# Two residual inputs: from Pool in one go to DVE in twelve pieces

## The chip, the core and the metric

The kernel runs on one core of a Trainium2 chip. A core has five engines that run their own instruction queues in order: TensorE (PE, matmuls and transposes), VectorE (DVE), ScalarE (ACT), GpSimd (Pool) and SyncE (SP), which issues most DMAs. They wait for each other through semaphores. The metric is the device time of one launch in microseconds (us).

## What is computed

Two blocks on a sequence of 256 tokens by 1024 channels, all in float32. The first (a convolution mixer and a mixture of 32 experts) ends in an RMS norm with weights `final_g`; its result is the input of the second. The second is two attention layers, each followed by a layer norm over the residual:

```python
for layer in range(DEPTH_2):
    if layer < N_A:
        y = mla_mixer(x, mla_w_in[layer], ...)
    else:
        if shared is None:
            shared = moba_shared_kv(x, moba_w_kv, cos_b, sin_b)
        y = moba_mixer(x, shared[0], shared[1], shared[2], moba_w_in[j], moba_w_o[j], cos_b, sin_b)
    x = layer_norm(ALPHA * x + y, ln_g[layer], ln_b[layer])
```

So each layer's input `x` is used twice: as the operand of its projections, and once more at its end as the residual `ALPHA * x`. The first layer's input (`x3` here) is the normed stream times `final_g`; the second's (`x4`) is the normed stream times `ln_g` plus `ln_b`.

## The kernel before

Tokens lie in two tiles of 128 (index `t`), channels in eight chunks of 128 (index `k`). Matmuls are made exact enough by splitting each float32 operand in a high part (rounded to the type `fp32r`) and the rest: `split` and `scaled_split` (L282 to L287) let ACT write the high part and DVE subtract it from the source. A product is then three matmuls: high by high, low by high, high by low. The weights are split in the same way, 1024 columns at a time, as `sh` (ACT) and `sl` (DVE); they are planned some chunks ahead of their use.

Each engine's order is set when the program is built, by a scheduler that the dependencies steer; `tc.issue_after(ins)` puts what is written in its block behind `ins`, where both are on the same engine.

The stages that matter here, in order of time:

- `to_channels` (L1175): PE transposes a token tile chunk by chunk into PSUM, the norm's weights are applied per channel on the way out (`xf`, by ACT for odd chunks, by DVE at L1192 for even ones), and `split` makes `xh` and `xl`. For the first layer this reads `x2` (the tile is called `x3` in the trace's program, shown as `x`), for the second `x4n`. So the projections don't need `x3` or `x4` themselves.
- First layer: keys' and values' latent rows (`pk`), their norm, the rotated key part `kr` (L1418 to L1423, copied at L1447 and transposed by PE at L1450), then six chunks of latent queries. `latent_q(i)` is one chunk: 24 matmuls into `pq`, `cqh` by ACT, `cql` by DVE (L287), the square `sqq` by ACT (L1431), which Pool adds up (L1433).
- Behind the latent queries `x2` is multiplied by `final_g` (`fg`, all rows alike) on Pool, L1455, two instructions of 128 x 1024. They stand behind Pool's norm power `kv_norm` in order. This is the residual of the first layer, read at its end (`out_norm`, L1392).
- Second layer: `x4n` is the normed stream; `to_channels` brings it to `xh`, `xl`, and the value projection `values(0)` begins as chunks arrive. Pool makes `x4` of `x4n` with two multiplies (L1546) and two adds (L1547) of 128 x 1024 by the rows `gb`.
- Then the key loop, eight chunks `m`: 24 matmuls, and `rope_t`: ACT copies the result to `raw`, `split` makes its high and low part (in `cqh`, on DVE the low part), and `rope_end` rotates the chunk before: two matmuls `pr`, DVE's `t1 = pr * sin` (L1260, shown as `t`), Pool's `raw = raw * cos` (L1261), DVE's sum `kn` (L1265). PE goes on with the next chunk ahead of `pr`.
- `values(1)`, and the second layer's attention and output.

The residual parts as written before:

```python
    with tc.issue_after(kv_norm.ins):
        for t in range(NT):
            nc.gpsimd.tensor_mul(x2[:, t, :], x2[:, t, :], fg[:, 0, :])
```

```python
    for t in range(NT):
        nc.gpsimd.tensor_mul(x4[:, t, :], x4n[:, t, :], gb[:, 0, :])
        nc.gpsimd.tensor_add(x4[:, t, :], x4[:, t, :], gb[:, 1, :])
```

Of the kernel before, what the change touches and what calls it, by code (L numbers as in the profile page):

```python
# [15 lines left out]
NT = 2  # L16
D = 1024
KD = 8
# [7 lines left out]
EPS = 1e-6  # L26
# [3 lines left out]
KVL = 256  # L30
# [5 lines left out]
V_C, V_AB, V_MIX, V_FFN, V_BIN, V_BDW, V_LNG, V_LNB, V_QN, V_KN, V_FIN = 0, 8, 56, 64, 72, 88, 96, 104, 112, 118, 120  # L36
# [5 lines left out]
T_MASK, T_COSA, T_SINA, T_COSB, T_SINB, T_R32, T_R64, T_COSK, T_SINK, T_N = (  # L42
    0, 256, 512, 768, 1024, 1280, 1408, 1536, 1600, 1664)
# [38 lines left out]
CQ_FIRST = 2  # L82
# [103 lines left out]
def build(tc, A, out, dbg=None, stop=None):  # L186
    nc = tc.nc
# [4 lines left out]
    def dump(name, t):  # L192
        if name in dbg:
            nc.sync.dma_start(dbg[name], t)
# [55 lines left out]
    vec = const.tile([P, V_ROWS], F32, name="vec")  # L250
    x2 = pre.tile([P, NT, D], F32, name="x2")
# [23 lines left out]
    def rsqrt(dst, ss, scale, eps):  # L275

        n = dst.shape[-1]
        nc.vector.tensor_scalar(dst, ss, scale, eps, op0=OP.mult, op1=OP.add)
        return nc.gpsimd.tensor_tensor(out=dst, in0=dst, in1=expn[:, :n], op=OP.pow)

    def split(hi, lo, src, eng=None):
        a = nc.scalar.copy(hi, src)  # L282
        return a, (eng or nc.vector).tensor_sub(lo, src, hi.bitcast(F32))  # L283

    def scaled_split(hi, lo, src, g):
        a = nc.scalar.activation(hi, src, AF.Identity, scale=g)
        return a, nc.vector.scalar_tensor_tensor(lo, src, g, hi.bitcast(F32), op0=OP.mult, op1=OP.subtract)  # L287
# [149 lines left out]
    for q in range(4):  # L437
        w = W.get()
        for i in range(2):
            m = 2 * q + i  # L440
# [76 lines left out]
    i = 0  # L517
# [107 lines left out]
    for k in range(KD):  # L625
# [3 lines left out]
        if k in (1, 2):  # L629
            h = k - 1  # L630
            c = slice(512 * h, 512 * h + 512)
# [174 lines left out]
    for t in range(NT):  # L806
        c = (P + 2 * E) * t
# [215 lines left out]
    x2 = xq.tile([P, NT, D], F32, name="x3")  # L1023
# [86 lines left out]
    for j in (1, 0):  # L1110
        for t in range(NT):
            last = scatter(done, t, False, True, (j,))

    pw = pme.tile([P, 512], F32, name="pw", tag="pgu")
    for i in range(WARM):
        with tc.issue_after(last.ins):
            last = mm(pw, ident, g2b[:, 0:512], True, True)
# [45 lines left out]
    def tab(a, n=T):  # L1163
        return tbl[:, a:a + n]
# [51 lines left out]
    def chunk_t(kk, xh, xl, pat=None):  # L1216
        wh, wl = S.get()
        if pat is not None:
            wh, wl = wh.rearrange(pat), wl.rearrange(pat)
        return proj_t(lambda k: wh[:, k], lambda k: wl[:, k], kk, xh, xl)  # L1220
# [28 lines left out]
    def rope_end():  # L1249

        dst, raw, rh, rl, rot, cos, sin = ropes.pop(0)
        pr = ps.tile([P, T], F32, name="pr", tag="pt", bufs=2)
        if rh is None:
            mm(pr, rot, raw, True, True)
        else:
            mm(pr, rot, rh, True, False)
            mm(pr, rot, rl, False, True)
        del rh, rl
        t1 = tw.tile([P, T], F32, name="t1", tag="xf")
        nc.vector.tensor_mul(t1, pr, sin)  # L1260
        nc.gpsimd.tensor_mul(raw, raw, cos)  # L1261
        n = P // len(dst)
        for i, d in enumerate(dst):
            r = slice(n * i, n * i + n)
            nc.vector.tensor_add(d, raw[r, :], t1[r, :])  # L1265
# [7 lines left out]
    def rope_t(dst, pin, rot, cos, sin):  # L1273

        raw = tw.tile([P, T], F32, name="raw", tag="raw")
        nc.scalar.copy(raw, pin)
        rh = rl = None
        if rot.dtype == F32R:
            spare.append(spare.pop(0))
            rh, rl = (cqh[:, 2 * spare[0] + i] for i in range(2))  # L1280
            split(rh, rl, raw)
        ropes.append((dst, raw, rh, rl, rot, cos, sin))
        if len(ropes) > 1:
            rope_end()

    mask = tab(T_MASK)

# [125 lines left out]
    for t in range(NT):  # L1413
        nc.scalar.activation(junk, pk[t][:, :KVL], AF.Square, accum_out=sts[:, 4 + t:5 + t])
        nc.scalar.copy(kr[:, t].rearrange("p a b -> p (a b)"), pk[t][:, KVL:KVL + RD])
        kv_norm = rsqrt(sts[:, 6 + t:7 + t], sts[:, 4 + t:5 + t], 1.0 / KVL, EPS)
        nc.vector.tensor_scalar(ckn[:, t, :], pk[t][:, :KVL], sts[:, 6 + t:7 + t], None, op0=OP.mult)
    sink = tab(T_SINK, 64).rearrange("p (t a b) -> p t a b", t=NT, a=2)  # L1418
    kr2v = kr2.rearrange("p t (a b) -> p t a b", a=2)
# [7 lines left out]

    def latent_q(i):
        pq = chunk_t(KD, xh, xl)
        scaled_split(cqh[:, i, :], cql[:, i, :], pq, vec[:, V_QN + i:V_QN + i + 1])  # L1430
        nc.scalar.activation(sqq[:, i, :], pq, AF.Square)  # L1431
        if 0 < i < 5:
            nc.gpsimd.tensor_add(sqq[:, 0, :], sqq[:, 0, :], sqq[:, i, :])  # L1433

    for i in range(CQ_FIRST):
        latent_q(i)
# [12 lines left out]
    for t in range(NT):  # L1449
        nc.tensor.transpose(ptk[0:96, P * t:P * t + P], kr4[:, t].rearrange("p a b -> p (a b)"), ident)  # L1450
    for i in range(CQ_FIRST, 6):
        latent_q(i)
    with tc.issue_after(kv_norm.ins):
        for t in range(NT):
            nc.gpsimd.tensor_mul(x2[:, t, :], x2[:, t, :], fg[:, 0, :])  # L1455
    dump("x3", x2)

    kR = ptk[64:96, :].unsqueeze(1).to_broadcast([RD, 4, T])
# [83 lines left out]
        to_channels((t,), x4n, v2[:, 0:8], v2[:, 16:24], xh, xl)  # L1542
    x4 = big("x4", shape=(NT, D))
    gb = rows(A["ln_g_2"][0:1, :], A["ln_b_2"][0:1, :])
    for t in range(NT):
        nc.gpsimd.tensor_mul(x4[:, t, :], x4n[:, t, :], gb[:, 0, :])  # L1546
        nc.gpsimd.tensor_add(x4[:, t, :], x4[:, t, :], gb[:, 1, :])  # L1547
    dump("x4", x4)


    r64 = cql[:, 0, 0:P]
# [9 lines left out]
    rotation[:] = ROT_B  # L1561
    values(0)
    for m in range(8):
        rope_t([kn[:, m, :]], chunk_t(KD, xh, xl), r64, tab(T_COSB), tab(T_SINB))
    values(1)
    rope_flush()
    ogh, ogl = big("ogh", F32R), big("ogl", F32R)
# [121 lines left out]
```

## Time and profile before

| | us |
|---|---|
| median of 3 runs (945.17 to 946.70) | 946.23 |
| the profiled execution | 945.95 |
| its span in the trace | 944.3 |
| PE busy | 869.0 (92%) |
| DVE busy | 526.6 (56%) |
| ACT busy | 361.2 (38%) |
| Pool busy | 58.2 (6%) |

Times in the rows below are counted from the span's start. A row of a timeline gives start, duration, engine, line, operation, output and inputs with their shapes, how many instructions are merged in it (x2), and in brackets how long the engine stood idle before and what released it. Shares over the whole span say little here, since the stages have different limits; the second block begins near 636 us.

### The profile page before, as it was taken

The page shows a single profiled execution, that of the slowest core. Times are in us where ns is not written, and L with a number is a line of the kernel's source. Part 1 is how long each engine was busy: PE and PEld are TensorE (multiplying, and loading weights), DVE is VectorE, ACT ScalarE, POOL GpSimd, SP SyncE. Part 2 cuts the span into 40 slices and gives each one's busy share as a digit, 9 for nine tenths or more (in the row PEclk, how much of TensorE's full clock was granted, in tenths as well). Part 3 has the DMA queues.
Part 4 walks back from the last instruction along what each step waited for, and adds up shares of the span by engine and source line. Part 5 has one row for each costly group of instructions (what it writes and reads, how often), then busy time and mean ns, then how long its engine had stood idle before and what let it go on. Part 6 is the DMA issues. An engine that isn't in the chain of part 4 may idle for free. (4 is left out here: it accounts for less than half of the span.)

```text
span 944.3 us, 15434 instructions
## 1 busy us (share of the span) xinstructions
PE 869.0 (92%) x6227; PEld 609.6 (65%) x6227; DVE 526.6 (56%) x1243; ACT 361.2 (38%) x788; POOL 58.2 (6%) x62
## 2 busy tenths in 40 slices
PE   4899879899999999999699999878999996999996
PEld 1597346665565555656356555538988874988975
DVE  2699965623343333334223342357777868758876
ACT  1455645412122121212012121145766735655761
POOL 0000210100000000000000000003100004110112
PEclk9899989999999999999899999999999998999998
DMA  9994968789999999999999999974432441624211
GB/s 372 411 389 191 406 249 317 323 362 426 427 427 428 426 427 426 427 426 430 422 428 425 426 429 425 425 311 159 170 140 91 179 178 45 255 102 179 90 45 45
DMA packets 23580, 289.44 MB, mean 307 GB/s; under 512 B 2736, under 2 KB 3408, under 8 KB 6096
## 3 DMA queue, kind: packets, MB, share of 16 engines
q1 hardware_dynamic: 21872, 282.29, 72.4%
q10 hardware_dynamic: 1632, 6.11, 1.8%
q8 instruction: 51, 0.84, 0.4%
q14 instruction: 25, 0.20, 0.1%
HBM read 287.34 MB, written 1.05 MB: 305 GB/s over the span
## 5 line engine op out<-in xcount | busy, mean ns | idle before, releaser
L197 PE MATMUL pgu<-w,xg 128*64 128x256 f32 x2048 | 233.5, 381 | 4.2 <-DMA w<-in_moe 4.2
L197 PEld LDWEIGHTS pgu<-w,xg 128*64 128x64 f32 x2048 | 145.6, 137 | 90.1 <-issue 20.8
L197 PE MATMUL pys<-w,hTe 128*64 128x512 f32 x512 | 116.1, 594 | 5.4 <-DMA w<-in_moe 2.5
L283 DVE TENSOR_TENSOR sl<-w,sh 128x1024 fp32r<-128x1024 f32 (+2 forms) x82 | 98.0, 1204 | 20.4 <-ACT sh L282 19.2
L282 ACT CAST sh<-w 128x1024 fp32r<-128x1024 f32 (+2 forms) x82 | 81.4, 1001 | 48.9 <-PE pj L197 46.0
L1012 DVE SCALAR_TENSOR_TENSOR yt<-pys,gs,g2b 64x512 f32<-64x512 f32 x64 | 48.0, 750 | 87.2 <-PE pys L197 86.2
L282 ACT CAST yh<-yt 64x512 fp32r<-64x512 f32 x64 | 39.6, 618 | 138.9 <-DVE yt L1012 137.3
L197 PE MATMUL pj<-xh,sh 128*128 128x256 f32 x304 | 86.6, 285 | 0.1
L197 PE MATMUL pj<-xl,sh 128*128 128x256 f32 x304 | 85.5, 281 | 0.0
L197 PE MATMUL pj<-xh,sl 128*128 128x256 f32 x304 | 85.3, 281 | 0.0
L197 PEld LDWEIGHTS pys<-w,hTe 128*64 128x64 f32 x512 | 36.2, 137 | 65.9 <-issue 54.5
L854 DVE TENSOR_TENSOR hid<-pgu,hid 128x256 f32<-128x256 f32 x32 | 13.6, 425 | 97.2 <-ACT hid L853 97.2
L853 ACT ACTIVATE hid<-pgu 128x256 f32<-128x256 f32 x32 | 12.3, 385 | 125.8 <-PE pgu L197 119.7
L197 PEld LDWEIGHTS pj<-xh,sh 128*128 128x128 f32 x304 | 57.1, 188 | 2.2 <-issue 1.6
L197 PEld LDWEIGHTS pj<-xl,sh 128*128 128x128 f32 x304 | 57.0, 188 | 1.8 <-issue 1.7
L197 PEld LDWEIGHTS pj<-xh,sl 128*128 128x128 f32 x304 | 57.1, 188 | 0.8 <-issue 0.8
L411 DVE SCALAR_TENSOR_TENSOR y<-up,wdw,y 128x256 f32<-128x256 f32 x120 | 54.9, 513 | 0.1
L283 DVE TENSOR_TENSOR yl<-yt,yh 64x512 fp32r<-64x512 f32 x64 | 44.0, 687 | 2.2 <-ACT yh L282 0.2
L197 PE MATMUL pu<-hh,wh 128*128 128x256 f32 x128 | 37.4, 292 | 2.7 <-ACT wh L282 2.7
L283 DVE TENSOR_TENSOR wl<-w,wh 128x512 fp32r<-128x512 f32 x48 | 33.2, 702 | 12.0 <-ACT wh L282 10.5
L282 ACT CAST wh<-w 128x512 fp32r<-128x512 f32 x48 | 29.3, 620 | 27.5 <-PE pu L197 20.4
L862 DVE COPY hTe<-pth 128x256 f32<-128x256 f32 x32 | 13.6, 425 | 44.6 <-PE pth L203 40.1
(343 smaller groups left out, 1579.2 us busy)
## 6 DMA issues: line engine op xcount, KB each, us to landing
w<-in_moe SPq DMA_DIRECT2D x95, 2048.0 KB, 32.0
w<-in_wst SPq DMA_DIRECT2D x32, 2048.0 KB, 8.7
w<-in_wst SPq DMA_DIRECT2D x5, 1152.0 KB, 5.1
w<-in_wst SPq DMA_DIRECT2D x2, 1536.0 KB, 11.2
wb<-in_wbd ACTq DMA_DIRECT2D x4, 512.0 KB, 7.0
w<-in_wst SPq DMA_DIRECT2D x2, 1024.0 KB, 22.6
w<-in_moe SPq DMA_DIRECT2D x4, 512.0 KB, 31.2
x<-in_x SPq DMA_DIRECT2D x1, 1024.0 KB, 11.5
```

The costliest lines, as they stand in the source:

```text
L197: ins = nc.tensor.matmul(o, l, r, start=start, stop=stop)
L282: a = nc.scalar.copy(hi, src)
L283: return a, (eng or nc.vector).tensor_sub(lo, src, hi.bitcast(F32))
L411: nc.vector.scalar_tensor_tensor(y[:, m, :], u, wdw[:, m, k:k + 1], y[:, m, :], op0=OP.mult, op1=OP.add)
L853: nc.scalar.activation(hid, pgu[:, 0:256], AF.Silu)
L854: nc.vector.tensor_mul(hid, pgu[:, 256:512], hid)
L862: nc.vector.tensor_copy(hT, pt.rearrange("p (q j s) -> p q j s", q=2, j=2))
L1012: nc.vector.scalar_tensor_tensor(yt[r, :], pys[r, :], gs[r, e % 2:e % 2 + 1], g2b[r, 512 * j:512 * j + 512], op0=OP.mult, op1=OP.mult)
```

## The change

Pool's six instructions of 128 x 1024 go. DVE does the same work in twelve pieces of 128 x 512: four multiplies of `x2`, one behind each of the latent queries 2 to 5, and for `x4` a multiply and an add in turn behind each of the eight keys' splits, with `issue_after` on that split's low part. To that end `rope_t` and `latent_q` now return it.

```diff
@@ rope_t
-        rh = rl = None
+        rh = rl = last = None
         if rot.dtype == F32R:
             spare.append(spare.pop(0))
             rh, rl = (cqh[:, 2 * spare[0] + i] for i in range(2))
-            split(rh, rl, raw)
+            last = split(rh, rl, raw)[1]
         ropes.append((dst, raw, rh, rl, rot, cos, sin))
         if len(ropes) > 1:
             rope_end()
+        return last
@@ latent_q
-        scaled_split(cqh[:, i, :], cql[:, i, :], pq, vec[:, V_QN + i:V_QN + i + 1])
+        a, v = scaled_split(cqh[:, i, :], cql[:, i, :], pq, vec[:, V_QN + i:V_QN + i + 1])
         nc.scalar.activation(sqq[:, i, :], pq, AF.Square)
         if 0 < i < 5:
             nc.gpsimd.tensor_add(sqq[:, 0, :], sqq[:, 0, :], sqq[:, i, :])
+        return v
@@
     for i in range(CQ_FIRST, 6):
-        latent_q(i)
-    with tc.issue_after(kv_norm.ins):
-        for t in range(NT):
-            nc.gpsimd.tensor_mul(x2[:, t, :], x2[:, t, :], fg[:, 0, :])
+        with tc.issue_after(latent_q(i).ins):
+            t, c = (i - CQ_FIRST) // 2, slice(512 * (i % 2), 512 * (i % 2) + 512)
+            nc.vector.tensor_mul(x2[:, t, c], x2[:, t, c], fg[:, 0, c])
@@
-    for t in range(NT):
-        nc.gpsimd.tensor_mul(x4[:, t, :], x4n[:, t, :], gb[:, 0, :])
-        nc.gpsimd.tensor_add(x4[:, t, :], x4[:, t, :], gb[:, 1, :])
-    dump("x4", x4)
+
+    def x4_part(m, after):
+
+        with tc.issue_after(after.ins):
+            t, c = m // 4, slice(512 * (m // 2 % 2), 512 * (m // 2 % 2) + 512)
+            if m % 2:
+                nc.vector.tensor_add(x4[:, t, c], x4[:, t, c], gb[:, 1, c])
+            else:
+                nc.vector.tensor_mul(x4[:, t, c], x4n[:, t, c], gb[:, 0, c])
@@
     for m in range(8):
-        rope_t([kn[:, m, :]], chunk_t(KD, xh, xl), r64, tab(T_COSB), tab(T_SINB))
+        x4_part(m, rope_t([kn[:, m, :]], chunk_t(KD, xh, xl), r64, tab(T_COSB), tab(T_SINB)))
+    dump("x4", x4)
```

The order of instructions on PE, ACT and SP is the same in both programs. On DVE at the latent queries (`x_5219` is `x2`, `rows` is `fg`, a row ending in x2 is two instructions), first before:

```order
L283 TENSOR_TENSOR sl<-w,sh 128x1024 x2
L287 SCALAR_TENSOR_TENSOR cql<-pj,vec,cqh 128x256 x2
L283 TENSOR_TENSOR sl<-w,sh 128x1024 x2
L287 SCALAR_TENSOR_TENSOR cql<-pj,vec,cqh 128x256 x2
L283 TENSOR_TENSOR sl<-w,sh 128x1024
```

Now, in the same place:

```order
L283 TENSOR_TENSOR sl<-w,sh 128x1024 x2
L287 SCALAR_TENSOR_TENSOR cql<-pj,vec,cqh 128x256
L1456 TENSOR_TENSOR x_5219<-x_5219,rows 128x512
L287 SCALAR_TENSOR_TENSOR cql<-pj,vec,cqh 128x256
L1456 TENSOR_TENSOR x_5219<-x_5219,rows 128x512
L283 TENSOR_TENSOR sl<-w,sh 128x1024 x2
L287 SCALAR_TENSOR_TENSOR cql<-pj,vec,cqh 128x256
L1456 TENSOR_TENSOR x_5219<-x_5219,rows 128x512
```

One piece stands directly behind each `cql` of the queries 2 to 5, ahead of the next `cql` or the next weight split. On DVE at the key loop's first steps (`cqh<-raw,cqh` is the low part of the split), before:

```order
L283 TENSOR_TENSOR cqh<-raw,cqh 128x256
L1260 TENSOR_TENSOR t_7156<-pr,tbl 128x256
L1265 TENSOR_TENSOR kn<-raw,t_7156 128x256
L283 TENSOR_TENSOR sl<-w,sh 128x1024
L283 TENSOR_TENSOR cqh<-raw,cqh 128x256
```

Now (`x_7010` is `x4`, `rows` is `gb`):

```order
L283 TENSOR_TENSOR cqh<-raw,cqh 128x256
L1554 TENSOR_TENSOR x_7010<-x4n,rows 128x512
L1260 TENSOR_TENSOR t_7155<-pr,tbl 128x256
L1265 TENSOR_TENSOR kn<-raw,t_7155 128x256
L283 TENSOR_TENSOR sl<-w,sh 128x1024
L283 TENSOR_TENSOR cqh<-raw,cqh 128x256
L1552 TENSOR_TENSOR x_7010<-x_7010,rows 128x512
```

A piece stands between each split of a raw key and the `t` that waits for PE's rotation; the same in all eight steps.

## Rows read from the trace of the kernel before

**Rows 1.** Waits of PE, 640 to 690 us: who for whom, total, times, longest
```profile
PE ptk L1450 <- DVE kr L1447: 2.5, 1, 2.5
PE pj L197 <- ACT sqq L1431: 0.3, 1, 0.3
```

**Rows 2.** Waits of PE, 780 to 850 us
```profile
PE pt L1182 <- DVE xf L1192: 3.8, 2, 2.0
PE pt L1182 <- ACT xf L1190: 2.4, 2, 2.1
PE pj L197 <- DVE xl L283: 1.6, 1, 1.6
```

**Rows 3.** Stretches: length, busy of PE, PEld, DVE, ACT, POOL, clock, DMA share, GB/s
```profile
786.00:796.00 10.00, 2.51 (x10) 1.21 (x8) 9.72 (x7) 2.27 (x7) 9.07 (x4) 0.81 0.06 25
796.00:800.00 4.00, 4.00 (x14) 3.02 (x14) 2.89 (x7) 3.81 (x10) 0.00 (x0) 0.62 0.00 0
800.00:806.00 6.00, 6.00 (x27) 4.87 (x26) 4.87 (x9) 4.71 (x9) 0.00 (x0) 1.00 0.47 147
```

**Rows 4.** Timeline, Pool and DVE, 646.5 to 653 us
```profile
646.82 4.75 POOL L1455 TENSOR_TENSOR x<-x,rows 128x1024 f32<-128x1024 f32 x2 [0.30 <-issue]
646.96 2.37 DVE L1423 TENSOR_TENSOR rows<-rows 128x64 f32<-128x64 f32 x1
...
652.57 0.25 DVE L1447 COPY kr<-rows 128x192 f32<-128x192 f32 x1
```

**Rows 5.** Timeline, Pool and DVE, the transposing stage of `x4n`
```profile
785.48 0.41 DVE L1192 TENSOR_SCALAR xf<-pt,v 128x128 f32<-128x128 f32 x1
785.66 4.72 POOL L1546 TENSOR_TENSOR x<-x4n,rows 128x1024 f32<-128x1024 f32 x2 [2.13 <-PE pj L197]
785.81 4.72 DVE L283 TENSOR_TENSOR xl<-xf,xh 128x128 fp32r<-128x128 f32 x2
...
795.33 0.41 DVE L1192 TENSOR_SCALAR xf<-pt,v 128x128 f32<-128x128 f32 x1
...
797.68 0.41 DVE L1192 TENSOR_SCALAR xf<-pt,v 128x128 f32<-128x128 f32 x1
```

**Rows 6.** Groups of DVE instructions up to 640 us: count, busy, mean ns
```profile
L605 DVE TENSOR_TENSOR x<-x,rg 128x512 f32<-128x512 f32 x3 | 2.0, 688 | 0.0
```

**Rows 7.** Timeline, DVE, Pool and PE, two steps of the key loop, and its last split
```profile
814.39 0.42 DVE L283 TENSOR_TENSOR cqh<-raw,cqh 128x256 fp32r<-128x256 f32 x1
814.88 0.75 POOL L1261 TENSOR_TENSOR raw<-raw,tbl 128x256 f32<-128x256 f32 x1 [2.23 <-DVE cqh L283]
814.91 0.40 PE L197 MATMUL pr<-cqh,cql 128*128 128x256 f32 x2
815.34 0.43 DVE L1260 TENSOR_TENSOR t<-pr,tbl 128x256 f32<-128x256 f32 x1 [0.54 <-PE pr L197]
815.87 0.43 DVE L1265 TENSOR_TENSOR kn<-raw,t 128x256 f32<-128x256 f32 x1
816.21 1.22 DVE L283 TENSOR_TENSOR sl<-w,sh 128x1024 fp32r<-128x1024 f32 x1
...
832.56 0.42 DVE L283 TENSOR_TENSOR cqh<-raw,cqh 128x256 fp32r<-128x256 f32 x1
```

**Rows 8.** Timeline, DVE, latent queries 3 and the weight splits behind
```profile
660.69 0.48 DVE L287 SCALAR_TENSOR_TENSOR cql<-pj,vec,cqh 128x256 fp32r<-128x256 f32 x1 [0.82 <-ACT cqh L286]
661.63 2.91 DVE L283 TENSOR_TENSOR sl<-w,sh 128x1024 fp32r<-128x1024 f32 x2 [0.45 <-ACT sh L282]
```

**Rows 9.** Timeline, DVE and PE: a weight split and PE's first use
```profile
799.02 1.23 DVE L283 TENSOR_TENSOR sl<-w,sh 128x1024 fp32r<-128x1024 f32 x1 [0.66 <-ACT sh L282]
801.39 0.39 PE L197 MATMUL pj<-sl,xh 128*128 128x512 f32 x1
```

**Rows 10.** Timeline, Pool and DVE, queries of the second layer
```profile
881.64 2.82 POOL L1261 TENSOR_TENSOR raw<-raw,tbl 128x256 f32<-128x256 f32 x2 [15.38 <-DVE cqh L283]
882.75 0.42 DVE L283 TENSOR_TENSOR cqh<-raw,cqh 128x256 fp32r<-128x256 f32 x1
```

More of the change, by code (lines that the diff above doesn't have):

```diff
@@ L1415, in build @@
         nc.scalar.copy(kr[:, t].rearrange("p a b -> p (a b)"), pk[t][:, KVL:KVL + RD])
-        kv_norm = rsqrt(sts[:, 6 + t:7 + t], sts[:, 4 + t:5 + t], 1.0 / KVL, EPS)
+        rsqrt(sts[:, 6 + t:7 + t], sts[:, 4 + t:5 + t], 1.0 / KVL, EPS)
         nc.vector.tensor_scalar(ckn[:, t, :], pk[t][:, :KVL], sts[:, 6 + t:7 + t], None, op0=OP.mult)
```

## Prediction

> **What bounds the kernel now.** I read the waits of TensorE (PE) first, then PE's busy time by stretch, then single instructions on DVE and Pool. The change moves work only in two stages of the second block, so the reader should ask of each: is PE, whose matmuls fill it, waiting there, and for whom?
>
> In the stage of the latent queries PE waits once for long, 2.5 us, for the DVE copy of `kr`; a further 0.3 us goes to ACT's `sqq` [rows 1]. In the stage that brings `x4n` to channel layout, PE waits 3.8 us for DVE's `xf`, 2.4 us for ACT's `xf` and 1.6 us for DVE's `xl` [rows 2]. By stretch [rows 3]: from 786 to 796 us PE is busy 2.51 of 10 us and its granted clock is 0.81 on average; from 796 to 800 us it is busy throughout but at 0.62, nearer to its lower level (1.2 GHz) than to the upper (2.4 GHz); from 800 us on it is busy without a break at 1.00. So DVE, which is busy 9.72 of those 10 us, bounds that stretch.
>
> DVE is not short of work capacity there, it is held. [rows 4]: Pool's two multiplies of L1455 run from 646.82 for 4.75 us; the DVE add L1423 on 64 columns, begun 0.14 us later, takes 2.37 us, and the `kr` copy two instructions behind it starts at 652.57. [rows 5]: Pool's L1546 starts at 785.66, and two `xl` subtractions on 128 columns take 4.72 us; when Pool has finished, a pair of channel chunks goes by in (797.68 - 795.33) / 2 = 1.18 us. What is held has both inputs in SBUF; the `xf` that reads PSUM keeps 0.41 us in the midst of it.
>
> **Part 1, Pool's multiply of x3 removed (L1455).** With Pool idle, L1423 ends near 647.2, then comes one weight split of 1.14 us, and `kr` is copied near 648.4, before PE's transposes come up. The 2.5 us wait of [rows 1] goes. Next late would be ACT's `sqq`, 0.3 us. I take 2.5 us; the ends are 2.2 (some of it stays) and 2.8 (both go).
>
> **Part 2, four DVE pieces of x3 added behind `cql`.** A multiply of two SBUF tiles on 128x512 has a row of the same form: 0.688 us [rows 6]. Instructions start 0.08 us before the one ahead has ended in the record (a 1.22 us split at 816.21 on DVE leaves 1.14 to its follower; `kn` of 0.43 at 815.87 has its follower at 816.21 [rows 7]), so a piece fills some 0.60 us. Behind the first and third piece stands a `cql` that today waits 0.82 us for ACT; behind the second and fourth a weight split that waits 0.45 us for ACT [rows 8]. The pieces lie in those waits but for 0.15 us twice, and those splits are made chunks ahead of PE. I take 0. If the cover were gone, 4 x 0.60 = 2.4 us.
>
> **Part 3, Pool's multiplies and adds of x4 removed (L1546, L1547).** Four pairs of chunks take 785.48 to 797.68 = 12.2 us; undisturbed 4 x 1.18 = 4.7. So DVE's chain comes 7.5 us earlier. PE can gain at most its idle 7.49 us plus 4.0 x (1 - 0.62) = 1.5 us of the slow clock: 9.0. What lies between is slack: of the weight splits that PE uses next, the nearest is begun at 799.02, ends 800.25 and is first read at 801.39 [rows 9]: 1.1 us. Thus 7.5 + 1.1 = 8.6 by this split, under the 9.0; I take 8.5, ends 7.5 and 9.0. It supposes that PE keeps the upper clock once its gaps are short; where it doesn't, the low end holds.
>
> **Part 4, eight DVE pieces of x4 added in the key loop.** This is where the change may cost. A step of the loop on DVE is: split of the raw key (`cqh`), wait for PE's rotation `pr`, `t`, `kn`, split of a weight. From 814.39 to 832.56 there are six steps, 3.03 us each [rows 7]. PE has no gap, so here is nothing to win. But its `pr` starts at 814.91 and the second of its two matmuls (near 815.03) needs the split that ends at 814.81: 0.22 us of slack. A DVE loop longer than PE's 3.03 us goes straight to PE.
>
> The piece starts where the split leaves off, 814.39 + 0.33 = 814.72, and lets `t` start at 815.32; `t` starts at 815.34 today. So on DVE alone it is free: it lies in the wait for `pr`. The cost comes by Pool: its `raw` multiply, at 814.88 today, has SBUF inputs too, and now finds DVE busy until 814.72 + 0.69 = 815.41. The same meeting is in [rows 10]: Pool's two `raw` multiplies start at 881.64 in the record and last 2.82 us, to 884.46, while DVE's last two-SBUF instruction ahead ran at 882.75 for 0.42, to 883.17; that leaves 0.65 us for each. So `raw` is done near 816.06 and `kn`, which needs it, starts at 816.10, where it starts at 815.87 today. Then 816.10 + 0.34 + 1.14 = 817.58 for the next split: a step of 3.19 us, 0.16 over PE's. Between the first split and the eighth are seven steps: 7 x 0.16 - 0.22 = 0.9 us. The ends: 0, if `raw` gets through beside the piece; with Pool's own 0.75 us instead of 0.65, 0.26 a step, 1.6 us. Below nothing is excluded, as PE has no gap.
>
> The page "SBUF — State Buffer" of the Trainium skill, section "Who interferes with whom", says that of a DVE instruction with two SBUF inputs and a GpSimd instruction that reads SBUF the first to issue blocks the other for all its length. By that rule the piece, 0.16 us ahead of Pool, blocks Pool and not the reverse, and the sum is the one above; were Pool ahead, it would be the first rival below. The trace agrees in both directions (2.37 us for L1423 behind Pool, 2.82 us for Pool's two behind DVE).
>
> **The sum.** The profiled execution took 945.95 us, its span 944.3. 945.95 - 2.5 - 8.5 + 0.9 = 935.85. It is 0.28 below the median of 946.23, so 936.1 as a median. The order of PE, ACT and SP is the same in both programs, so nothing else is costed. Less than 0.2% (1.9 us) can't be told from no change here.
>
> **The rivals.**
> First, *Pool goes first in the key loop*. Then Pool has 814.88 to 815.63, the piece starts at 815.63, `t` at 816.24, `kn` at 816.77, the next split at 818.25: 3.86 us a step, 0.83 over. 7 x 0.83 - 0.22 = 5.6 us, and 945.95 - 2.5 - 8.5 + 5.6 + 0.28 = 940.8. For it: the margin is 0.16 us. Against: DVE's queue has the piece directly behind the split, and Pool must first be told that the split is done.
> Second, *half the gain goes into a new wait*, the weights: PE comes 11 us earlier, the loads may not. Against: in 786 to 800 us DMA is nearly idle (0.06 and 0.00 [rows 3]), so loads wait for free buffers, and those come free earlier too. It would cost up to half of 8.5: 936.1 + 4.2 = 940.3.
> Third, on the other side, *Pool isn't what holds DVE* in these stages, but something that ends at the same time. Then PE's gaps stay, nothing is gained, and the pieces cost what part 4 gives: 0.9 to 5.6 us, so 947.1 to 951.8, about 949. It decides from the point where the gain is below the key loop's cost, 0.9 us. Against: in two stages, with different tiles, the held instructions are freed as Pool ends, and the next ones run at 1.18 us a pair at once.
> That the change doesn't do what it says is excluded by the order: Pool's six are gone, DVE's twelve stand behind the splits.
>
> **How the numbers follow.** Forecast 936.1 with 0.84; first rival 0.07; second 0.06; third 0.03. The range takes the ends of the terms: 945.95 - 2.8 - 9.0 + 0 + 0.28 = 934.4 and 945.95 - 2.2 - 7.5 + 1.6 + 0.28 = 938.1; with half of the 1.5 us by which the runs shown differ, 933.8 to 938.8. It leaves out the 0.16 of the rivals. Faster by over 0.2%: the forecast and the first two rivals, 0.97; within 0.2%: 0.01; slower: 0.02, most of the third.
>
> **What would show it.** Part 1: PE's wait for `kr` is gone and L1423 is back near 0.2 us. Part 3: no `xl` over 0.5 us, the transposing stage about 8.5 us shorter, the granted clock near 1.00 in it. Part 4: splits of the key loop 3.1 to 3.3 us apart, small PE waits for DVE before `pr`, Pool's `raw` multiplies longer than 1 us. Part 2: no PE wait over 0.5 us between the latent queries. The forecast is wrong if `xl` is still held with Pool idle, if the steps are 3.8 us apart, or if PE waits for weights behind the transposing stage.

## The result, and the profile after

The changed kernel takes 934.86 us (median of 4 runs, 932.90 to 935.73); the kernel before took 945.75 us beside it (945.17 to 946.70). The ratio is 0.9881, with a 95% interval of 0.9863 to 0.9900: faster by 10.9 us between the medians (the ratios here and below come from all runs of the two kernels and aren't quite the quotients of the medians). In two later comparisons the same kernel came to 0.9869 (0.9853 to 0.9886) and 0.9853 (0.9828 to 0.9879). The profiled execution shown here took 935.17 us, with a span of 933.5 us.

To see where the time went I cut both spans at five marks that both traces have: the start of the second block's first norm power on Pool (L279), that of the power ahead of `x4n` (L279), DVE's first and eighth split of a raw key, and its next split, of a query. The figures are differences of start times, in us.

| stretch | before | after | difference | term of the prediction |
|---|---|---|---|---|
| start to the second block's first power | 643.49 | 644.29 | +0.80 | none |
| to `x4n`'s power: latent queries, first attention | 133.60 | 130.36 | -3.24 | parts 1 and 2: -2.5 |
| to the first key split: transposing stage | 34.33 | 25.87 | -8.46 | part 3: -8.5 |
| to the eighth key split: key loop | 21.14 | 21.98 | +0.84 | part 4: +0.9, with the next row |
| to the first query split: values(1) | 14.36 | 14.12 | -0.24 | |
| to the end | 97.38 | 96.88 | -0.50 | none |
| span | 944.3 | 933.5 | -10.8 | -10.1 |

The first row and the last are no work of the change. The first mark stood at 641.9 us in two more executions of the changed kernel, 2.4 us earlier, with the same instructions; and in all the other traces below the last stretch is 96.8 to 97.0 us, so it is before's that is 0.5 long. The rows between them sum to -11.1 us.

The page's first lines, busy time of each engine with its share of the span:

```profile
PE 867.7 (93%) x6227; PEld 609.9 (65%) x6227; DVE 520.6 (56%) x1255; ACT 360.3 (39%) x788; POOL 46.6 (5%) x56
```

DVE has twelve instructions of some 0.6 us more than before and yet 6.0 us less of busy time (526.6 before): it is held less. Pool has six instructions less.

**Latent queries.** The only wait of PE from 640 to 690 us, which answers to [rows 1]:

```profile
PE pj L197 <- ACT sqq L1432: 0.2, 1, 0.2
```

The wait for `kr` is gone. The timeline of DVE shows why (start, duration, engine, line, output and inputs); it answers to [rows 4], with all lines one to two further down:

```profile
647.63 0.21 DVE L1424 TENSOR_TENSOR rows<-rows 128x64 f32<-128x64 f32 x1
647.77 1.22 DVE L283 TENSOR_TENSOR sl<-w,sh 128x1024 fp32r<-128x1024 f32 x1
648.90 0.25 DVE L1449 COPY kr<-rows 128x192 f32<-128x192 f32 x1
...
657.71 0.48 DVE L287 SCALAR_TENSOR_TENSOR cql<-pj,vec,cqh 128x256 fp32r<-128x256 f32 x1 [0.22 <-ACT cqh L286]
658.11 0.68 DVE L1456 TENSOR_TENSOR x<-x,rows 128x512 f32<-128x512 f32 x1
658.71 1.22 DVE L283 TENSOR_TENSOR sl<-w,sh 128x1024 fp32r<-128x1024 f32 x1
```

The add on 64 columns takes 0.21 us where it took 2.37, and `kr` is copied at 648.90 instead of 652.57. The `cql` behind a piece still waits for ACT, 0.22 us where it was 0.82 [rows 8]: the piece lies in that wait.

**Transposing stage.** Waits of PE from 770 to 850 us, which answer to [rows 2]:

```profile
PE pj L197 <- ACT xh L282: 0.9, 1, 0.9
PE pt L1182 <- ACT xf L1190: 0.8, 2, 0.5
```

Then the stretches of [rows 3], with the same columns (length, busy of PE, PEld, DVE, ACT, POOL, clock, DMA share, GB/s):

```profile
786.00:796.00 10.00, 9.97 (x46) 7.68 (x46) 8.59 (x17) 9.39 (x19) 0.00 (x0) 1.00 0.27 90
796.00:800.00 4.00, 4.00 (x37) 4.00 (x36) 2.29 (x3) 2.57 (x5) 0.00 (x0) 1.00 0.99 381
```

and DVE's timeline, which answers to [rows 5]:

```profile
783.02 0.41 DVE L1192 TENSOR_SCALAR xf<-pt,v 128x128 f32<-128x128 f32 x1
...
784.54 0.72 DVE L283 TENSOR_TENSOR xl<-xf,xh 128x128 fp32r<-128x128 f32 x2
...
787.71 0.41 DVE L1192 TENSOR_SCALAR xf<-pt,v 128x128 f32<-128x128 f32 x1
```

Of the 7.8 us of waits that [rows 2] shows the 5.4 for DVE are gone, and of ACT's 2.4 for `xf` 0.8 are left; the 0.9 for ACT's `xh` isn't new: PE waited the same 0.9 us for it before, in a row of that view that [rows 2] doesn't show (`PE pj L197 <- ACT xh L282: 0.9, 1, 0.9`). Two `xl` take 0.72 us together where they took 4.72, and the four pairs go by in 787.71 - 783.02 = 4.69 us instead of 12.2. The granted clock is 1.00 where it was 0.81 and 0.62: PE, with no long gaps ahead, stays at its upper level (2.4 GHz). So 7.8 - 0.8 = 7.0 us of waits went, and 4.0 x (1 - 0.62) = 1.5 us of clock: 8.5, against the 8.46 of the table.

**Key loop.** One step on DVE and Pool, which answers to [rows 7]:

```profile
803.66 0.42 DVE L283 TENSOR_TENSOR cqh<-raw,cqh 128x256 fp32r<-128x256 f32 x1
804.00 0.69 DVE L1552 TENSOR_TENSOR x<-x,rows 128x512 f32<-128x512 f32 x1
804.22 1.07 POOL L1261 TENSOR_TENSOR raw<-raw,tbl 128x256 f32<-128x256 f32 x1 [2.07 <-DVE cqh L283]
804.60 0.42 DVE L1260 TENSOR_TENSOR t<-pr,tbl 128x256 f32<-128x256 f32 x1
805.32 0.42 DVE L1265 TENSOR_TENSOR kn<-raw,t 128x256 f32<-128x256 f32 x1 [0.31 <-POOL raw L1261]
805.67 1.22 DVE L283 TENSOR_TENSOR sl<-w,sh 128x1024 fp32r<-128x1024 f32 x1
806.80 0.42 DVE L283 TENSOR_TENSOR cqh<-raw,cqh 128x256 fp32r<-128x256 f32 x1
```

The piece starts 0.34 us behind the split, and `t` no later than before: 0.94 us behind the split, 0.95 in [rows 7]. Pool's multiply, 0.75 us before, now takes 1.07; `kn` waits 0.31 us for it and starts 1.66 us behind the split instead of 1.48. A step is 806.80 - 803.66 = 3.14 us.

### The profile page after: what moved, and what is told of

Same layout as the page of the kernel before. It is cut to its first block, busy times and chain, and to the rows that moved or that the text cites. A ratio compares the mean times of both kernels' runs of the same rounds, so it can differ in the third digit from the quotient of the medians.

```text
span 933.5 us, 15438 instructions
## 1 busy us (share of the span) xinstructions
PE 867.7 (93%) x6227; PEld 609.9 (65%) x6227; DVE 520.6 (56%) x1255; ACT 360.3 (39%) x788; POOL 46.6 (5%) x56
## 5 line engine op out<-in xcount | busy, mean ns | idle before, releaser
L197 PE MATMUL pgu<-w,xg 128*64 128x256 f32 x2048 | 233.5, 381 | 4.0 <-DMA w<-in_moe 4.0
L197 PEld LDWEIGHTS pgu<-w,xg 128*64 128x64 f32 x2048 | 145.9, 137 | 89.8 <-issue 20.6
L197 PE MATMUL pys<-w,hTe 128*64 128x512 f32 x512 | 116.1, 595 | 5.4 <-DMA w<-in_moe 2.5
L283 DVE TENSOR_TENSOR sl<-w,sh 128x1024 fp32r<-128x1024 f32 (+2 forms) x82 | 95.6, 1173 | 19.0 <-ACT sh L282 17.9
L282 ACT CAST sh<-w 128x1024 fp32r<-128x1024 f32 (+2 forms) x82 | 81.3, 998 | 51.3 <-PE pj L197 47.6
L282 ACT CAST yh<-yt 64x512 fp32r<-64x512 f32 x64 | 39.5, 617 | 139.0 <-DVE yt L1012 137.4
L197 PE MATMUL pj<-xh,sh 128*128 128x256 f32 x304 | 86.7, 285 | 0.0
L197 PE MATMUL pj<-xl,sh 128*128 128x256 f32 x304 | 85.8, 282 | 0.0
L197 PE MATMUL pj<-xh,sl 128*128 128x256 f32 x304 | 85.5, 281 | 0.0
L197 PEld LDWEIGHTS pys<-w,hTe 128*64 128x64 f32 x512 | 36.3, 137 | 65.9 <-issue 54.5
L197 PEld LDWEIGHTS pj<-xh,sh 128*128 128x128 f32 x304 | 57.2, 188 | 1.7 <-issue 1.6
L197 PEld LDWEIGHTS pj<-xl,sh 128*128 128x128 f32 x304 | 57.1, 188 | 1.8 <-issue 1.7
L197 PEld LDWEIGHTS pj<-xh,sl 128*128 128x128 f32 x304 | 57.1, 188 | 0.8 <-issue 0.8
L282 ACT CAST wh<-w 128x512 fp32r<-128x512 f32 x48 | 29.2, 618 | 27.8 <-PE pu L197 21.5
L197 PE MATMUL pu<-hh,wh 128*128 128x256 f32 x128 | 37.2, 291 | 2.7 <-ACT wh L282 2.7
L283 DVE TENSOR_TENSOR wl<-w,wh 128x512 fp32r<-128x512 f32 x48 | 32.8, 693 | 12.2 <-ACT wh L282 11.3
## 6 DMA issues: line engine op xcount, KB each, us to landing
w<-in_wst SPq DMA_DIRECT2D x2, 1536.0 KB, 11.1
```

What stands on the lines that cost most here:

```text
L197: ins = nc.tensor.matmul(o, l, r, start=start, stop=stop)
```

## Experiments

**The two halves alone.** e1 is the changed kernel with Pool's old code for `x4`, e2 the changed kernel with Pool's old code for `x3`. e1, against the kernel after:

```diff
-            if m % 2:
-                nc.vector.tensor_add(x4[:, t, c], x4[:, t, c], gb[:, 1, c])
-            else:
-                nc.vector.tensor_mul(x4[:, t, c], x4n[:, t, c], gb[:, 0, c])
+    for t in range(NT):
+        nc.gpsimd.tensor_mul(x4[:, t, :], x4n[:, t, :], gb[:, 0, :])
+        nc.gpsimd.tensor_add(x4[:, t, :], x4[:, t, :], gb[:, 1, :])
...
```

> Only the four pieces of x3 are on DVE; x4 stays on Pool as before. Theory (Pool's instructions hold DVE's, and each stage pays for itself): the gain of the latent-query stage alone, 3.1 us by the two traces, so 942.6 against 945.75; the transposing stage keeps its xl of over 2 us. Rival (the x3 part gives nothing by itself, since PE waits later anyway): 945.5 to 946.

Measured: 943.51 us (941.57 to 944.05) against 945.64, ratio 0.9964 (0.9948 to 0.9979), 0.9 over the 942.6 expected. The stretch of the latent queries takes 130.37 us, as after (130.36), and PE's waits in the transposing stage stand as in [rows 2]:

```profile
PE pt L1182 <- DVE xf L1192: 3.8, 2, 2.0
PE pt L1182 <- ACT xf L1190: 2.4, 2, 2.1
```

e2, against the kernel after:

```diff
...
-        with tc.issue_after(latent_q(i).ins):
-            t, c = (i - CQ_FIRST) // 2, slice(512 * (i % 2), 512 * (i % 2) + 512)
-            nc.vector.tensor_mul(x2[:, t, c], x2[:, t, c], fg[:, 0, c])
+        latent_q(i)
+    with tc.issue_after(kv_norm.ins):
+        for t in range(NT):
+            nc.gpsimd.tensor_mul(x2[:, t, :], x2[:, t, :], fg[:, 0, :])
```

> Only the eight pieces of x4 are on DVE; x3 stays on Pool as before. Theory: 8.6 us less in the transposing stage, 0.5 to 0.9 more in the key loop, so 937.7 to 938.1. Rival (the two parts share one gain, so that either alone gives nearly all): 935 to 936.

Measured: 937.89 us (936.79 to 938.64), ratio 0.9911 (0.9895 to 0.9928). The transposing stage takes 25.89 us (after: 25.87), the key loop 21.99 (21.98), the latent queries 134.54, 0.9 more than before with a granted clock of 0.92 from 646 to 668 us, and there PE waits nearly as in [rows 1]:

```profile
PE ptk L1452 <- DVE kr L1449: 2.4, 1, 2.4
```

The halves are independent: each gives its own stretch what it has in the whole, and the two shortfalls of the ratio, 0.0036 and 0.0089, sum to 0.0125, the whole's 0.0119 to 0.0147.

**The work on no engine.** e3 leaves both products and the sum out (the residuals are the unscaled streams) and so the transfer of the rows `gb` too:

```diff
-        with tc.issue_after(latent_q(i).ins):
-            ...
+        latent_q(i)
...
-    gb = rows(A["ln_g_2"][0:1, :], A["ln_b_2"][0:1, :])
-    def x4_part(m, after):
-        ...
+    x4 = x4n
```

> Both residual inputs' work is left out on every engine (the norm weights of x3 and x4 are not applied to the residual, and their rows are not loaded for x4). What is left when neither Pool nor DVE has it. Theory: after's time less the key loop's price, 934.9 - 0.6 = 934.3 (933.7 to 934.9), key loop steps 3.03 us. Rival (the DVE pieces cost their full 12 x 0.6 = 7.2 us somewhere): 927 to 928.

Measured: 931.86 us (931.32 to 935.21), ratio 0.9857 (0.9832 to 0.9881). By stretch: latent queries 130.39 us against 130.36 after, so the four `x3` pieces cost nothing (part 2); key loop 21.34 against 21.98, so the `x4` pieces cost some 0.6 us there, of which values(1) gives back 0.2 as in the table above (14.34 us against 14.12). Two more things went that I hadn't expected. The transposing stage takes 25.17 instead of 25.87 us: the two transfers of `gb` that ACT issues amid the transposes (0.33 us of its queue each) are left out, and PE's wait of 0.9 us for `xh` with them. And the second block began 2.0 us earlier, which varies from one execution to the next; it makes up most of the miss in the profiled execution.

**Pool writes only.** e4 is the kernel before with Pool's six instructions replaced by 18 that read nothing and write the same tiles (values that mean nothing); the transfer of `gb`, which nothing reads then, is left out too:

```diff
-            nc.gpsimd.tensor_mul(x2[:, t, :], x2[:, t, :], fg[:, 0, :])
+            for q in range(3):
+                nc.gpsimd.memset(x2[:, t, :], 0.25 + q)
...
-    gb = rows(A["ln_g_2"][0:1, :], A["ln_b_2"][0:1, :])
...
-        nc.gpsimd.tensor_mul(x4[:, t, :], x4n[:, t, :], gb[:, 0, :])
-        nc.gpsimd.tensor_add(x4[:, t, :], x4[:, t, :], gb[:, 1, :])
+        for q in range(6):
+            nc.gpsimd.memset(x4[:, t, :], 0.25 + q)
```

> The kernel before, with Pool's six multiplies and adds replaced by memsets of the same tiles in the same places of Pool's queue (18 of 128 x 1024, so that Pool is busy for about as long): it writes as much but reads nothing; the two inputs' values are left out. Theory (what holds DVE is Pool reading SBUF): L1423 0.2 us, no xl over 0.6 us, PE's waits of 2.5 and 7.8 us gone, time near 934.3. Rival (what holds DVE is Pool being busy, its writes, or something that ends with its instructions): xl and L1423 stay at 2 us and more, time near 945.75.

Measured: 944.72 us in a single execution, where before had 945.64 (944.56 to 948.98); by the count from the second block's first power 301.18 us, against 300.81. Pool and DVE in the two stages:

```profile
644.80 5.43 POOL L1456 MEMSET x<- 128x1024 f32 x6
645.28 0.21 DVE L1423 TENSOR_TENSOR rows<-rows 128x64 f32<-128x64 f32 x1
645.42 1.22 DVE L283 TENSOR_TENSOR sl<-w,sh 128x1024 fp32r<-128x1024 f32 x1
646.55 3.79 DVE L1447 COPY kr<-rows 128x192 f32<-128x192 f32 x1
...
781.38 9.89 POOL L1547 MEMSET x<- 128x1024 f32 x11
781.54 9.87 DVE L1537 TENSOR_SCALAR x4n<-z,mv,rs 128x256 f32<-128x256 f32 x1
791.33 0.39 DVE L1537 TENSOR_SCALAR x4n<-z,mv,rs 128x256 f32<-128x256 f32 x1
791.65 0.28 DVE L283 TENSOR_TENSOR xl<-xf,xh 128x128 fp32r<-128x128 f32 x1
```

The theory's first half holds: the add on 64 columns keeps its 0.21 us and the weight split its 1.22 in the midst of Pool's writes, and no `xl` is held. What I hadn't foreseen is that DVE instructions with one input in SBUF are: the copy of `kr` takes 3.79 us (after: 0.25) and ends 0.11 us behind Pool's last write (645 to 650 us), and of two writes of `x4n` the first takes 9.87 us and ends 0.14 us behind the last of Pool's eleven in that stretch, the second 0.39. So the time didn't fall, for a reason of its own, and the expected 934 was wrong. That Pool isn't what holds DVE (the third rival) falls all the same: which DVE instructions are held changes with what Pool does, and they come free when Pool is done.

**What a step of the key loop pays for.** e5 is the changed kernel without Pool's `raw` multiply in the key loop:

```diff
-        nc.gpsimd.tensor_mul(raw, raw, cos)
+        if not key_loop:
+            nc.gpsimd.tensor_mul(raw, raw, cos)
...
```

> The kernel after, without Pool's multiply of `raw` by the cosine table in the eight steps of the key loop; that factor is left out of the keys, so the work on Pool is missing there and nothing else. My theory: a step is 3.14 us instead of 3.02 because Pool's multiply takes 1.07 us and is done only 0.61 us after the piece is, so that `kn` waits 0.31 us for it. Without it `kn` follows `t` at once, VectorE's work in a step is under TensorE's 3.03 us, the weight splits come 3.02 to 3.05 us apart, and from the first to the seventh `pr` it is 18.1 to 18.3 us instead of 18.70: 0.4 to 0.6 us under the kernel after. Rival: the piece's own 0.60 us on VectorE is the price, however Pool stands; then the splits stay 3.12 to 3.16 us apart and the time is that of after.

Measured: 932.91 us (931.70 to 935.56) against 945.27, ratio 0.9872 (0.9840 to 0.9905); by the time alone this can't be told from after. The trace can tell it: from the first to the eighth split it is 21.06 us (21.97 to 21.98 in three traces of after), 3.01 a step, as fast as before (21.14). One step on DVE:

```profile
804.89 0.42 DVE L283 TENSOR_TENSOR cqh<-raw,cqh 128x256 fp32r<-128x256 f32 x1
805.23 0.68 DVE L1555 TENSOR_TENSOR x<-x4n,rows 128x512 f32<-128x512 f32 x1
805.91 0.42 DVE L1260 TENSOR_TENSOR t<-pr,tbl 128x256 f32<-128x256 f32 x1
806.37 0.43 DVE L1266 TENSOR_TENSOR kn<-raw,t 128x256 f32<-128x256 f32 x1
```

The piece is there, 0.68 us long, and `kn` starts 1.48 us behind the split, as in the kernel before. The kernel before has Pool's multiply and no piece (21.14 us), e5 has the piece and no multiply (21.06 us): neither alone lengthens the loop, the two together do (21.98 us). So DVE's added 0.60 us cost nothing by themselves; the price is the wait for Pool that they bring. The rival, that the piece itself is the price, falls.

e7 puts each piece behind `kn` instead:

```diff
-        x4_part(m, rope_t([kn[:, m, :]], chunk_t(KD, xh, xl), r64, tab(T_COSB), tab(T_SINB)))
+        rope_t([kn[:, m, :]], chunk_t(KD, xh, xl), r64, tab(T_COSB), tab(T_SINB))
+        if m:
+            x4_part(m - 1, last_kn[0])
...
```

> The kernel after with each piece of the key loop put one place later, behind `kn` instead of behind the split of `raw`, so that VectorE's order in a step is `kn`, piece, weight split, sl, t. My theory, that a piece costs by the work of Pool that it meets: Pool's multiply of `raw` now stands beside the next weight split and not behind a piece, but `kn` still waits for the two in turn, so a step is 3.05 to 3.15 us and the time within 0.4 us of the kernel after. Rival: Pool's multiply meets no work that keeps it waiting, VectorE's 2.75 us of work in a step is under TensorE's 3.03, and the steps are 3.02 to 3.03 us with the time about 0.5 us under the kernel after.

Measured: 934.22 us (932.51 to 935.77), ratio 0.9874 (0.9855 to 0.9893), the time of after. The steps from the second on are 3.14 us (3.13 to 3.15); the first, which has no weight split, is 2.43, so the loop is 21.28 us. One of them on Pool and DVE:

```profile
805.80 0.42 DVE L283 TENSOR_TENSOR cqh<-raw,cqh 128x256 fp32r<-128x256 f32 x1
806.13 1.22 DVE L283 TENSOR_TENSOR sl<-w,sh 128x1024 fp32r<-128x1024 f32 x1
806.36 1.60 POOL L1261 TENSOR_TENSOR raw<-raw,tbl 128x256 f32<-128x256 f32 x1 [1.54 <-DVE cqh L283]
807.27 0.42 DVE L1260 TENSOR_TENSOR t<-pr,tbl 128x256 f32<-128x256 f32 x1
808.00 0.42 DVE L1265 TENSOR_TENSOR kn<-raw,t 128x256 f32<-128x256 f32 x1 [0.31 <-POOL raw L1261]
```

As expected, Pool's multiply now lies behind the weight split (1.60 us long, ending 0.61 us after the split does at 807.35), and `kn` waits the same 0.31 us. The rival, steps of 3.02 to 3.03 us, falls. Be the DVE instruction ahead of Pool a piece or a weight split, Pool's multiply ends 0.60 to 0.61 us behind it.

e6 makes each piece 1024 columns wide, the same result twice over:

```diff
-            t, c = m // 4, slice(512 * (m // 2 % 2), 512 * (m // 2 % 2) + 512)
+            t, c = m // 4, slice(0, D)
```

> The kernel after with each piece of `x4` in the key loop 1024 columns wide instead of 512 (each token tile's product and sum are made twice over, the values are the same): twice the added work on VectorE. My theory, a price that starts once VectorE's chain in a step is longer than TensorE's 3.03 us: the piece takes about 1.22 us instead of 0.68, `kn` starts about 2.2 us after the split instead of 1.6, a step becomes 3.6 to 3.7 us, and from the first to the seventh `pr` it is 3 to 4 us more than in the kernel after, so about 938 to 939 us. Rival: the pieces lie in idle time of VectorE and the 0.11 us by which a step grew has another source; then doubling them adds less than 1 us.

Measured: 934.36 us (933.70 to 937.97), ratio 0.9895 (0.9860 to 0.9929), lower than expected. The steps did grow: six of the seven are 3.17 to 3.84 us, the other, which has no weight split, 2.68, and the key loop takes 24.98 us, 3.0 more than after, the low end of what I had named. The rival, less than 1 us, falls. But the scheduler had put the piece behind `kn`, so the order isn't that of after, and it was Pool that came first there:

```profile
804.32 0.42 DVE L1265 TENSOR_TENSOR kn<-raw,t 128x256 f32<-128x256 f32 x1
804.55 0.79 POOL L1261 TENSOR_TENSOR raw<-raw,tbl 128x256 f32<-128x256 f32 x1 [3.04 <-DVE cqh L283]
804.66 1.76 DVE L1554 TENSOR_TENSOR x<-x4n,rows 128x1024 f32<-128x1024 f32 x1
```

The piece takes 1.76 us where the loop's first piece, which Pool's multiply follows, takes 1.22 (at 797.32 us): 0.54 us held behind Pool, the order of the first rival. Of the 3.0 us, 0.7 is given back in values(1) (13.42 us against 14.12), where DVE has idle time; counted from the second block's first power the kernel takes 290.91 us, 1.8 over after. The run shows that a piece twice as wide no longer fits into a step; what it costs by itself can't be read from it, because of the other order.

**Two attempts at a better version.** e8 moves the pieces out of the key loop, the first behind the last key's split, two and five behind weight splits of values(1):

```diff
-        x4_part(m, rope_t([kn[:, m, :]], chunk_t(KD, xh, xl), r64, tab(T_COSB), tab(T_SINB)))
+        low = rope_t([kn[:, m, :]], chunk_t(KD, xh, xl), r64, tab(T_COSB), tab(T_SINB))
+    x4_part(0, low)
+    later = [lambda low, m=m: x4_part(m, low) for m in range(1, 8)]
+    S.hook = [(), (), later[:2], later[2:]]
...
```

`S.hook` names, for each of the next four weight splits, the pieces that are written behind it.

> The kernel after with the eight pieces of `x4` taken out of the key loop's steps: the first behind the last key's weight split, two and five behind the weight splits that values(1) makes after the keys, where VectorE is idle for 0.4, 1.5 and 3.0 us in the trace of after. My theory: what the key loop lost (0.53 us from the first to the seventh `pr`) was lost to the pieces alone, so its steps go back to TensorE's 3.02 us and the kernel is about 0.5 us under the one after, 934.3 against 934.9. Rivals: VectorE's idle time after the keys doesn't cover the pieces, a later weight split comes late and the time is that of after or up to 2 us above it; or the step's growth stays, because it doesn't come from the pieces.

e9 does the same, and has ACT issue the transfers of `gb` behind values(0):

```diff
-    gb = rows(A["ln_g_2"][0:1, :], A["ln_b_2"][0:1, :])
+    gb = big("rows", shape=(2, D))
...
+    with tc.issue_after(values(0).ins):
+        for i, ap in enumerate((A["ln_g_2"][0:1, :], A["ln_b_2"][0:1, :])):
+            nc.scalar.dma_start(gb[:, i, :], ap.to_broadcast([P, D]))
```

> The kernel e8 (no pieces of `x4` in the key loop's steps but the first, behind the last key), and besides the two transfers that load the scale and offset rows of `x4` are issued by ScalarE behind values(0), where it idles 1.40 us in the trace of after, and no longer amid the transposes. Reason: with these transfers left out (e3), the stretch from the second block's last rsqrt to the key loop's first split was 25.17 us against 25.87; each issue takes ScalarE 0.33 us, and TensorE waits 0.9 us for its `xh` there. Expected: that stretch 25.1 to 25.4 us, the key loop as in e8 (21.4 us from the first split to the eighth), the whole about 1 us under the kernel after, span counted from the second block's first rsqrt 287.9 to 288.2 us against 289.1. Rival: the 0.70 us in e3 came from the data not being moved, or ScalarE's wait is only put elsewhere; then the stretch stays at 25.8 us and only the key loop's 0.5 us is left.

Each had the changed kernel beside it on the same chip:

> The changed kernel again, unedited, as the measure for the two runs beside it: 934 to 936 us.

> The changed kernel again, unedited, on the same chip as the run beside it: 932 to 936 us; counted from the second block's first rsqrt to the end, 289.0 to 289.3 us.

| | us, median (range) | ratio to before | from first power | transposing stage | key loop | values(1) |
|---|---|---|---|---|---|---|
| e0, after again | 933.01 (932.67 to 934.88) | 0.9869 (0.9853 to 0.9886) | 289.08 | 25.89 | 21.97 | 14.13 |
| e8 | 933.87 (932.35 to 935.50) | 0.9877 (0.9857 to 0.9897) | 288.56 | 25.90 | 21.43 | 14.34 |
| e0b, after again | 932.48 (932.16 to 934.80) | 0.9853 (0.9828 to 0.9879) | 288.95 | 25.88 | 21.98 | 14.14 |
| e9 | 933.86 (931.58 to 935.53) | 0.9860 (0.9836 to 0.9885) | 288.00 | 25.57 | 21.13 | 14.35 |

In the traces both do what they were made for. In e8 the key loop gives back 0.54 us and values(1) takes 0.21 more, with the pieces in DVE's idle time there:

```profile
820.97 1.23 DVE L283 TENSOR_TENSOR sl<-w,sh 128x1024 fp32r<-128x1024 f32 x1 [0.61 <-ACT sh L282]
822.12 0.68 DVE L1554 TENSOR_TENSOR x<-x,rows 128x512 f32<-128x512 f32 x1
822.72 0.68 DVE L1556 TENSOR_TENSOR x<-x4n,rows 128x512 f32<-128x512 f32 x1
...
825.52 1.29 DVE L1556 TENSOR_TENSOR x<-x4n,rows 128x512 f32<-128x512 f32 x2
```

These two stretches make up 0.33 of the 0.52 us by which e8 is shorter than the kernel after from the first power on.

e9 gives back 0.31 us more in the transposing stage (I expected 0.5 to 0.8; its values(0) is also interleaved with the transposes in another way). Counted from the second block's first power e9 is 0.95 us under after. The times don't show it: their medians are above that of after, and the intervals overlap almost wholly. So neither is shown to beat the changed kernel; a gain of half a microsecond to one is under what the start of the second block varies by (641.3 to 644.8 us over these traces).

## Why the prediction was right

The forecast was 936.1 us, in a range of 933.8 to 938.8; the time was 934.86. It was right by its steps, as the stretches and the experiments show, and most sizes hold. That the median came within 1.3 us is in part luck: the start of the second block, which belongs to no part, alone varies by 3.5 us over the traces here.

**Part 1, Pool's multiply of x3.** Predicted -2.5 with ends 2.2 and 2.8; the stretch lost 3.24 us, beyond the end. The mechanism is as told; the size was read from the wrong column. I took PE's wait from the list of waits, which counts from the modelled end of the last matmul. What a gap costs is read from start to start. In the kernel before:

```profile
649.78 0.60 PE L1442 MATMUL ptc<-cst,rows 128*128 128x128 f32 x4
652.88 0.42 PE L1450 MATMUL ptk<-cst,kr 128*96 128x128 f32 x2 [2.49 <-DVE kr L1447]
653.06 0.36 PE L197 MATMUL pj<-xh,sh 128*128 128x256 f32 x1
```

and after:

```profile
650.58 0.60 PE L1444 MATMUL ptc<-cst,rows 128*128 128x128 f32 x4
651.02 0.38 PE L1452 MATMUL ptk<-cst,kr 128*96 128x128 f32 x2
651.16 0.36 PE L197 MATMUL pj<-xh,sh 128*128 128x256 f32 x1
```

From the first transpose to the first matmul behind them it was 653.06 - 649.78 = 3.28 us and is 0.58: 2.70, where the list says 2.49. From there to PE's transpose of `v2r` behind the stage (677.53 before, 675.16 after) it was 24.47 us and is 24.00, another 0.47: the wait for `sqq` halved (0.31 to 0.15 us), and two pauses at the start of a latent chunk, which the list of waits doesn't show, closed (at 656.20 and 661.93 us the matmuls stood 0.35 and 0.30 us apart instead of 0.12). With the halved wait they come to 0.57, so this is right to 0.1 us. Why these two stood there isn't shown; they came while ACT and DVE were catching up with the late `kr`.

**Part 2, the four pieces.** Predicted 0. e3, without them, has the same stretch to 0.03 us; a `cql` behind a piece still waits 0.22 us.

**Part 3, Pool's work on x4.** Predicted -8.5 from 7.5 us of DVE's chain and 1.1 us of slack; measured -8.46. The chain came to 12.2 - 4.69 = 7.5. The weight split of [rows 9] and its first read show the slack used up:

```profile
789.11 1.23 DVE L283 TENSOR_TENSOR sl<-w,sh 128x1024 fp32r<-128x1024 f32 x1 [0.66 <-ACT sh L282]
790.39 0.50 PE L197 MATMUL pj<-sl,xh 128*128 128x512 f32 x1
```

Counted from the power ahead of `x4n`, the split starts 7.5 us earlier than before and the read 8.6; the read comes 0.05 us behind the split's end, 1.14 before. So this term's split into 7.5 and 1.1 holds, and not the total alone. The condition on the clock held too. The other waits that PE has left are ACT's, 1.7 us; the 0.9 us for `xh` go with the two transfers that ACT issues there, since the wait is missing in e3 and in e9.

**Part 4, the eight pieces.** Predicted +0.9, measured +0.84 to the eighth split, of which values(1) gives back 0.24: +0.60. The step was put at 3.19 us and is 3.14, because Pool's multiply needs 0.60 us behind the piece (804.22 + 1.07 = 805.29, the piece ends at 804.69) and not 0.65, and `kn` starts as it ends. The 0.65 was the mean of two multiplies that [rows 10] merges: taken singly, the first ends at 883.77, 0.60 behind DVE's 883.17, and the second takes 0.72 with nothing ahead of it. Seven steps at 0.11 over PE's 3.03, less 0.22 of slack, make 0.55; the slack is what the table shows as values(1)'s -0.24: ahead of the eighth split PE's `pr` starts 0.38 us behind the split (819.74 and 819.36), 0.62 before (830.11 and 829.49). That the price is the wait for Pool and not DVE's own time is shown by e5 (the wait gone, the piece kept: 3.01 a step) and e7 (the piece elsewhere, the wait kept: 3.14).

The page "SBUF — State Buffer" of the Trainium skill, section "Who interferes with whom", says that whichever of the two engines issues first keeps the other out for all its instruction. The traces agree in both directions: Pool's 128x256 multiply takes 1.07 us behind a piece and 1.60 behind a weight split, DVE's 1024-wide piece 1.76 us instead of 1.22 behind Pool.

**The rivals.** Pool never came first in the key loop of the kernel after: all eight of its multiplies start 0.22 to 0.23 us behind a piece's start, and take 1.06 or 1.07 us. No wait for weights took the gain: PE has no wait for a DMA between 770 and 850 us, though the loads now fall into the transposing stage's end (DMA share 0.99 from 796 to 800 us, against 0.00 in [rows 3]). That Pool isn't the cause is refuted by e1 and e2, where the waits come back in the stage whose Pool work comes back and in no other, and by e4.

**The sum.** For the profiled execution the terms gave 935.85, and it took 935.17, 0.7 less: 0.74 by part 1 and 0.3 by part 4 with values(1), less the 0.3 by which the first and the last stretch, which belong to no part, lengthened it. The rest of the 1.2 us between forecast and median is the place of the profiled execution among the runs, 0.28 below the median before and 0.31 above it after. The range has a slip: with half of 1.5 us on either side its terms give 933.7 to 938.9, not 933.8 to 938.8, which changes nothing here.

## What to carry to other kernels

Work that an idle engine does "for free" isn't free when it reads the memory that the bound engine's feeder reads (or, in e4, only writes it): look for an instruction of the feeder that takes ten times its usual time and ends with the other engine's, and price the move by the stage's waits and by the clock that follows them. On the other side, when work is moved to the feeder, follow not only its own queue but every instruction of the other engine that the moved piece now stands ahead of, and who waits for that; here the whole price was 0.11 us a step by that wait. Read the cost of a gap on PE from start to start of its matmuls, not from the list of waits, which was 0.2 us short for one gap and left out two others.

## What the runs showed of the hardware

Pool's writes hold DVE too, but other instructions than Pool's reads do. In e4, while Pool only wrote, DVE's instructions on two SBUF tiles kept their time (0.21 us on 64 columns, 1.22 on 1024), and a float32 copy of 192 columns took 3.79 us instead of 0.25, a scale-and-shift of 256 columns 9.87 us where the next, alone, took 0.39. In the kernel before, with Pool reading, the two-input instructions were the ones held (2.37 and 4.72 us, [rows 4, 5]). The same section of the Trainium skill says that copies and tensor-scalar operations can enter a mode that uses the shared ports and so contend; the two rows agree with that.

How long a hold lasted differed too. In e4 the copy and the scale-and-shift weren't held by one write, some 0.95 us each, but through the rest of a row of six and of eleven that followed each other. In the kernel before, Pool's multiplies followed each other as closely, and yet one held DVE instruction came free with each. The first of Pool's two ends at 649.25, `kr`'s add 0.08 us behind it, and only the weight split behind is held through the second:

```profile
646.82 2.43 POOL L1455 TENSOR_TENSOR x<-x,rows 128x1024 f32<-128x1024 f32 x1 [0.30 <-issue]
649.26 3.39 DVE L283 TENSOR_TENSOR sl<-w,sh 128x1024 fp32r<-128x1024 f32 x1
```

In the transposing stage four held `xl` end 0.14 to 0.15 us behind Pool's four instructions, one behind each. Why the one lets something in and the other doesn't isn't shown; what was held was of another form too.

One step of the key loop, the second or third, was 0.25 to 0.45 us longer than its neighbours in e1, e3, e4 and e8, with `kn` starting 0.46 us after the end of `t` where 0.10 is usual [rows 7], and no row that says what for. It stays open; it makes the 21.34 of e3 and the 21.43 of e8 that much longer than seven usual steps would be.
